# The first values of two head groups, summed together block by block in six banks

## The chip, the cores and the metric

The kernel runs on one core of a Trainium2 chip. The metric is the device time of one execution in microseconds (us). Before the change it is 1462.3 us, the median of three runs between 1461.91 and 1462.77.

The engines are named as the profile names them: PE is TensorE (matrix products and transposes) and PEld its weight loads; DVE is VectorE, ACT is ScalarE, POOL is GpSimd, and SP (SyncE) issues most of the transfers. Each engine takes its instructions strictly in the order of the program, and they wait for each other through semaphores. Transfers go from the memory outside the core (HBM) to the on-chip memory (SBUF); products are summed in PSUM, which has eight banks of 512 float32 columns.

## The reference, and what is computed

One layer of an encoder on x (1024 tokens by 1024 features): token mixing with two head groups side by side, cross-attention into 256 memory tokens, and a squared-ReLU MLP. Only its first lines matter here:

```python
h = rmsnorm(x, g_mix_pre[l])
proj = h @ w_in[l]          # fq fk fv f_logit cq ck cv
y_fox = forgetting_attention(fq, fk, fv, f_logit)
y_chk = chunked_relpos_attention(cq, ck, cv, rel_bias[l])
```

The change concerns the first products of the program: the values of four heads of each group, that is 256 columns of cv (called group 1, "chk") and 256 columns of fv with the 8 columns of the forget gate beside them (group 0, "fox", 264 columns), for all 1024 tokens.

## The kernel before, in words

**Numbers in two parts.** A float32 operand is split into a hi part (a copy rounded to the format that PE takes at full rate) and a lo part (the operand less its hi part). A product is then three products, hi·hi, hi·lo and lo·hi, summed in one bank; mm3 (L191 to L195) writes these three.

**Halves and blocks.** The 1024 tokens are two halves (th 0 and 1) of 512, each four token blocks (kb) of 128. The 1024 features over which is summed are eight contraction blocks (kc) of 128. A bank holds one token block of one group; it takes 8 contraction blocks of 3 products, 24 products. The first half's values are 4 token blocks of 2 groups, 192 products, and the second half's as many.

**The first half** does not wait for the norm. x is loaded transposed (xT), multiplied by the gain gmix alone and split (gained_hi on ACT at L1648, gained_lo on DVE at L1651). The norm's factor, one number per token, is applied when the values leave their bank: value_leave (L341) copies the hi part on ACT (L348), for group 0 the gate columns too (L350, fcol), and takes the lo part on DVE (L351).

The factor comes from sums of squares. For the first half, square (L1633) squares each block on ACT (L1636) and adds it up on DVE (L1638); when all eight are added, four small products with a column of 1/1024 (ssx, L1697) sum over the features, DVE adds epsilon (L1698) and POOL raises to the power -0.5 (L1699). For the second half ACT squares four row blocks of x with a running sum (L1705), and POOL does the rest (L1716, L1717). To scale the transposed x, the factors are turned into rows: transposes on PE (rr, L1725) and copies on ACT into rrows (L1726).

**The order of the first half.** Group 1 goes first: its four banks are filled side by side, contraction block by contraction block. Then group 0 bank by bank (values, L335): token block 0, ssx, token block 1, the eight turning transposes rr, token blocks 2 and 3. Group 1's banks are emptied while group 0's are filled. Weight pieces are split in value_split: group 1's hi parts on POOL (L316), group 0's on ACT (L318), all lo parts on DVE (L319).

**The second half and the norm.** normed (L1738) scales x on DVE (scaled, L1732), splits off the hi part on ACT (L1733) and takes the lo part on DVE (rest, L1736), for the eight blocks of the second half and then for those of the first half again, which later products use. Calls of value_leave stand at given places between these blocks. Group 1 is then summed over its four token blocks at once, and group 0 bank by bank.

**Transfers.** One piece of the first weights goes on ACT's queue, the rest on SP's: gmix, the two halves of the first xT pair, a weight piece, two xT pairs, a weight piece, the last xT pair, then group 0's weights with the rows of x between them.

**What follows.** stock holds the weights that come next: stock.load(3) issues three loads, stock.split_now(2) splits the first two (wq and wk: hi on ACT at L449, lo in two pieces on POOL at L458). attention_phase then writes the rest from a plan that keeps its own clock and starts at zero there; its first products are q, which read the first half's normalised x and wq. All of this part is written out by hand, so each engine's order is the order of the text.

**Warm-up.** 17 transposes of a constant (L1628) run on PE while the first data is on its way.

Of the kernel before, what the change touches and what calls it, by code (L numbers as in the profile page):

```python
# [14 lines left out]
F32 = mybir.dt.float32  # L15
# [120 lines left out]
def build(ctx, tc, nc, out, t):  # L136
# [155 lines left out]
    def value_raw(g, i, tag=None, halves=False):  # L292


        n, (a, b) = 264 if g == 0 else 256, VPARTS[g][i]
        shape = [P, b - a, n]
        raw = (wp.tile(shape, F32, tag="wraw", bufs=3, name=f"wrawv{g}{a}") if tag is None else
               p1.tile(shape, F32, tag=tag, bufs=2, name=f"wrawv{g}{a}"))
        src = t[f"w_v{g}"][a * P * n:b * P * n].rearrange("(p k n) -> p k n", p=P, n=n)
        if not halves:  # L300
            nc.sync.dma_start(raw, src)
            return raw
        h = (b - a) // 2
        return raw, [lambda j=j, q=q: q.dma_start(raw[:, j:j + h, :], src[:, j:j + h, :])
                     for j, q in ((0, nc.scalar), (h, nc.sync))]

    def value_split(g, raw, i, pieces=1, between=None):
        k, shape = raw.shape[1], list(raw.shape)
        if g == 1:
            wh, wl = (wp.tile(shape, F32R, tag=x, bufs=2, name=f"{x}v{i}") for x in ("whi", "wlo"))  # L310
        else:
            wh, wl = (u4(f"{x}v0{i}", shape) for x in ("whi", "wlo"))
        n = k // pieces
        for j in range(0, k, n):
            if between:
                nc.gpsimd.tensor_copy(wh[:, j:j + n, :], raw[:, j:j + n, :])  # L316
            else:
                nc.scalar.activation(wh[:, j:j + n, :], raw[:, j:j + n, :], AF.Copy)  # L318
            nc.vector.tensor_sub(wl[:, j:j + n, :], raw[:, j:j + n, :], f(wh[:, j:j + n, :]))  # L319
            if between and j == 0:  # L320
                between()
        return [(wh[:, j, :], wl[:, j, :]) for j in range(k)]

# [6 lines left out]

    def value_part(ps, w, kb, kc):
        act, cs = hT[kb // 4], slice((kb % 4) * P, (kb % 4 + 1) * P)
        mm3(ps, act.hi(kc, cs), act.lo(kc, cs), *w[kc], kc == 0, kc == KC - 1)

    def values(g, w, kb, tag):  # L335
        ps = value_bank(g, kb, tag)
        for kc in range(KC):
            value_part(ps, w, kb, kc)
        return ps
# [1269 lines left out]
    with tc.manual_schedule():  # L1609
        xt, xloads = load_pair(0, 0, True)  # L1610
        raw, wloads = value_raw(1, 0, halves=True)
        xT, raw1 = {0: [xt], 1: []}, [raw]
        gmix = const.tile([P, KC], F32, name="gmix")
        wloads[0]()
        early = const.tile([P, 1], F32, name="early")
        nc.scalar.activation(early, mhalf[:, 0:1], AF.Copy)
        nc.sync.dma_start(gmix, t["g_mix_pre"])
        xloads[0]()
        xloads[1]()
        wloads[1]()  # L1620
        xT[0] += [load_pair(0, 1), load_pair(0, 2)]
        raw1.append(value_raw(1, 1))
        xT[0].append(load_pair(0, 3))
        raw0 = [value_raw(0, 0)]
        vs = {g: value_tiles(g) for g in (1, 0)}
        warm = mm_tile([P, 4, P], "warm", "tr")
        for n in range(17):
            nc.tensor.transpose(warm[:, n % 4, :], ident, ident)  # L1628
# [11 lines left out]
        w1, w0, xr = [], [], []  # L1640

        def row(b):
            xr.append(p1.tile([P, D], F32, tag="sp", bufs=5, name=f"x{b}"))
            nc.sync.dma_start(xr[-1], t["x"][b * P:(b + 1) * P, :])

        def gained_hi(kc):

            nc.scalar.activation(hT[0].hi(kc), xT[0][kc // 2][:, kc % 2, :], AF.Copy, scale=gmix[:, kc:kc + 1])  # L1648
# [8 lines left out]

        gained_hi(0)
        w1 += value_split(1, raw1[0], 0, 2, lambda: (gained_lo(0), gained(1)))
        for kc in (2, 3):  # L1660
            gained(kc)
        for kc in (0, 1):
            square(kc)
        gained(4)
        w1 += value_split(1, raw1[1], 1, 2, lambda: gained(5))
        for kc in (2, 3):
            square(kc)
        for kc in (6, 7):
            gained(kc)
        first = [value_bank(1, kb, ("mm", "tr")[kb // 2]) for kb in range(4)]  # L1670
        for kc in range(KC):
            if kc > 1:
                for kb in range(4):
                    value_part(first[kb], w1, kb, kc)
                continue

            for n in range(3):
                for kb in range(4):
                    cs = slice(kb * P, (kb + 1) * P)
                    x = (hT[0].lo if n == 2 else hT[0].hi)(kc, cs)  # L1680
                    nc.tensor.matmul(first[kb], x, w1[kc][n == 1], start=kc == 0 and n == 0, stop=False)
        raw0 += [value_raw(0, 1, "bias"), None]
        for kc in (4, 5):
            square(kc)
        w0 += value_split(0, raw0[0], 0)
        w0 += value_split(0, raw0[1], 1)
        for b in (4, 5):
            row(b)
        raw0[2] = value_raw(0, 2)
        w0 += value_split(0, raw0[2], 2)  # L1690
        for kc in (6, 7):
            square(kc)
        ps0 = [values(0, w0, 0, "s")]
        rcols = [small.tile([P, 4], F32, tag="rs4", bufs=4, name=f"rx{th}") for th in range(2)]
        ps = mm_tile([P, 4], "ssx", "pv")
        for b in range(4):
            nc.tensor.matmul(ps[:, b:b + 1], sq[0][:, b * P:(b + 1) * P], o1024, start=True, stop=True)  # L1697
        nc.vector.tensor_scalar(rcols[0], ps, EPS, None, op0=ALU.add)  # L1698
        nc.gpsimd.tensor_tensor(rcols[0], rcols[0], mhalf[:, 0:4], op=ALU.pow)  # L1699

        ss1 = small.tile([P, 4], F32, tag="rs4", bufs=4, name="ssx1")
        junk = p1.tile([P, D], BF16, tag="o2", bufs=2, name="junk")

        def row_squares(b):
            nc.scalar.activation(junk, xr[b - 4], AF.Square, scale=1.0 / 32.0, accum_out=ss1[:, b - 4:b - 3])  # L1705

        for b in (6, 7):
            row(b)
        for p in range(4):
            xT[1].append(load_pair(1, p))  # L1710
        for b in (4, 5, 6):
            row_squares(b)
        row_squares(7)
        for kb in range(4):
            value_leave(1, kb, first[kb])
        nc.gpsimd.tensor_scalar(rcols[1], ss1, EPS, None, op0=ALU.add)  # L1716
        nc.gpsimd.tensor_tensor(rcols[1], rcols[1], mhalf[:, 0:4], op=ALU.pow)  # L1717
        ps0.append(values(0, w0, 1, "s"))
        value_leave(0, 0, ps0[0])

        rrows = p1.tile([P, 2, HT], F32, tag="bias", bufs=2, name="rrows")
        for th in (1, 0):
            tr = mm_tile([P, 4, P], f"rr{th}", "pv")
            for b in range(4):
                nc.tensor.transpose(tr[:, b, :], rcols[th][:, b:b + 1].to_broadcast([P, P]), ident)  # L1725
            nc.scalar.activation(rrows[:, th, :], tr.rearrange("p a b -> p (a b)"), AF.Copy)  # L1726
        nc.sync.dma_start(bfgt, t["b_fgt"])
# [10 lines left out]
        def normed(th, kcs, then={}):  # L1738

            for kc in kcs:  # L1740
                scaled(th, kc)
                if kc > kcs[0]:
                    rest(th, kc - 1)
                if kc in then:
                    then[kc]()
            rest(th, kcs[-1])

        for kb in (2, 3):
            ps0.append(values(0, w0, kb, "mm"))
# [717 lines left out]
```

## Time and profile before

| What | Value |
|---|---|
| Median of the runs | 1462.3 us |
| Profiled execution, span from first to last instruction | 1459.5 us |
| PE busy | 1447.7 us, 99% |
| DVE, ACT, POOL busy | 996.0, 820.7 and 421.0 us |
| First product of the values | 5.07 us |
| First product of the second half's values | 33.70 us |
| First product of q | 56.82 us |
| Mean granted clock of PE | 0.998 |

The profiled execution has a span of 1459.5 us; the runs' times count 2.8 us more around it. A row of the timeline gives start and duration in us, the engine, the line of the kernel, the operation, output and inputs by their names, and how many instructions are merged in it; in brackets stands how long the engine was idle before and what ended that. A row of the time table gives the stretch, its length, and the busy time of each engine with the number of its instructions, then the granted clock of PE (1.00 is full speed), the busy share of the DMA engines and their GB/s. A group row gives the summed busy time in us, the mean of one in ns, and the idle time before.

### The profile page before, as it was taken

The numbers are of one execution on the slowest core, as the hardware profiler recorded it, in microseconds if no ns is written. First come the engines' busy times: TensorE is split into PE (matmuls) and PEld (weight loads), VectorE is DVE, ScalarE is ACT, GpSimd is POOL, SyncE is SP. The second block draws the span as 40 slices with busy tenths as digits, with TensorE's granted clock in tenths as the row PEclk, the third lists the DMA queues.
The fourth block names the chain that finished last, engine by engine and source line by source line (L and its number), as shares of the span: only waits on it lengthen the run. The fifth ranks groups of instructions, "written<-read, shape, count | busy, mean of one in ns | idle before, by whom it ended". The sixth has DMA issues, their size and how long they took to land.

```text
span 1459.5 us, 21037 instructions
## 1 busy us (share of the span) xinstructions
PE 1447.7 (99%) x7265; PEld 1222.2 (84%) x7265; DVE 996.0 (68%) x1704; ACT 820.7 (56%) x1437; POOL 421.0 (29%) x520
## 2 busy tenths in 40 slices
PE   9999999999999999999999999999999999999998
PEld 8988888888889888888788888888888888888886
DVE  6777777767668847976873687765555666655576
ACT  6567677766677836555653465545555543444442
POOL 1245456555455301521332414343322000000021
PEclk9999999999999999999999999999999999999999
DMA  7132324321325584552541637754444785445565
GB/s 276 49 95 72 83 67 140 86 82 46 95 58 161 174 314 173 187 179 86 181 138 44 200 132 260 258 196 159 159 151 161 286 318 185 140 149 190 186 246 202
DMA packets 88987, 232.17 MB, mean 159 GB/s; under 512 B 10649, under 2 KB 14753, under 8 KB 88881
## 3 DMA queue, kind: packets, MB, share of 16 engines
q1 hardware_dynamic: 88736, 230.57, 47.6%
q8 instruction: 57, 0.93, 0.3%
q14 instruction: 50, 0.40, 0.1%
q10 hardware_dynamic: 144, 0.26, 0.1%
HBM read 167.30 MB, written 55.11 MB: 152 GB/s over the span
## 4 chain that ended last, share of the span: by engine, by line
PE 96%; DVE 2%; DMA 1%; ACT 1%; issue 0%; SPq 0%; DVEq 0%; ACTq 0%
PE pv L754 4%; PE fx L194 4%; PE fx L193 4%; PE fx L195 4%; PE ptr L711 4%; PE px L194 3%; PE fy L193 3%; PE px L195 3%; PE fy L195 3%; PE px L193 3%; PE fy L194 3%; PE mq L195 2%; PE q L193 2%; PE q L195 2%; PE q L194 2%; PE yw L193 2%
## 5 line engine op out<-in xcount | busy, mean ns | idle before, releaser
L717 DVE TENSOR_TENSOR phl<-ptr,phl 128x512 fp32r<-128x512 f32 (+1 forms) x152 | 92.5, 616 | 31.5 <-ACT phl L720 30.5
L2163 ACT ACTIVATE whif<-ra 128x1024 fp32r<-128x1024 f32 x37 | 39.2, 1061 | 130.3 <-PE fy L194 62.6
L2165 DVE TENSOR_TENSOR wlof<-ra,whif 128x1024 fp32r<-128x1024 f32 x37 | 45.3, 1225 | 91.7 <-ACT whif L2163 91.7
L720 ACT ACTIVATE phl<-ptr 128x512 fp32r<-128x512 f32 (+1 forms) x152 | 79.8, 540 | 40.3 <-PE ptr L711 38.5
L2285 POOL TENSOR_SCALAR rf<-sf 128x1 f32<-128x1 f32 x7 | 7.9, 1130 | 321.7 <-ACT jf L2266 321.4
L754 PE MATMUL pv<-phl,vs 128*128 128x512 f32 (+1 forms) x304 | 85.2, 366 | 0.2 <-DVE phl L717 0.2
L193 PE MATMUL fx<-vhif,whif 128*128 128x512 f32 x168 | 65.4, 389 | 0.0
L195 PE MATMUL fx<-vhif,wlof 128*128 128x512 f32 x168 | 65.4, 389 | 0.0
L194 PE MATMUL fx<-vlof,whif 128*128 128x512 f32 x168 | 65.4, 389 | 0.0
L754 PEld LDWEIGHTS pv<-phl,vs 128*128 128x128 f32 x304 | 55.2, 188 | 11.0 <-DVE phl L717 0.7
L2050 POOL TENSOR_TENSOR sc<-wf,wf 128x512 f32<-128x512 f32 x14 | 23.1, 1652 | 141.1 <-DMA wf<-in_w_ff 122.6
L768 POOL TENSOR_TENSOR o<-o 64x256 f32<-64x256 f32 x64 | 47.8, 747 | 53.1 <-DVE o L766 29.0
L193 PE MATMUL k<-hT_hi,whik 128*128 128x512 f32 x128 | 53.6, 419 | 0.0
L766 DVE TENSOR_TENSOR o<-pv,o 64x512 f32<-64x512 f32 x64 | 44.0, 688 | 13.5 <-ACT o L771 12.1
L193 PE MATMUL q<-hT_hi,whiq 128*128 128x512 f32 x128 | 51.6, 403 | 0.0
L193 PE MATMUL mq<-h2T_hi,whimq 128*128 128x512 f32 x128 | 51.4, 401 | 0.0
L195 PE MATMUL mq<-h2T_hi,wlomq 128*128 128x512 f32 x128 | 50.2, 392 | 0.2 <-DVE wlomq L455 0.2
L195 PE MATMUL k<-hT_hi,wlok 128*128 128x512 f32 x128 | 50.3, 393 | 0.0
L194 PE MATMUL k<-hT_lo,whik 128*128 128x512 f32 x128 | 50.3, 393 | 0.0
L195 PE MATMUL q<-hT_hi,wloq 128*128 128x512 f32 x128 | 50.2, 392 | 0.0
L194 PE MATMUL q<-hT_lo,whiq 128*128 128x512 f32 x128 | 50.2, 392 | 0.0
L194 PE MATMUL mq<-h2T_lo,whimq 128*128 128x512 f32 x128 | 50.1, 392 | 0.1
(696 smaller groups left out, 5014.5 us busy)
## 6 DMA issues: line engine op xcount, KB each, us to landing
ra<-gd SPq DMA_DIRECT2D x56, 512.0 KB, 3.8
wg<-in_w_ff SPq DMA_DIRECT2D x56, 512.0 KB, 5.6
wf<-in_w_ff SPq DMA_DIRECT2D x38, 512.0 KB, 3.9
gd<-s SPq DMA_DIRECT2D x48, 256.0 KB, 2.1
wrawmq<-in_w_mq SPq DMA_DIRECT2D x16, 512.0 KB, 4.3
gd<-u SPq DMA_DIRECT2D x32, 256.0 KB, 2.2
gd<-g SPq DMA_DIRECT2D x25, 256.0 KB, 2.2
wrawq<-in_w_qk SPq DMA_DIRECT2D x8, 512.0 KB, 4.4
```

What stands on the lines that cost most here:

```text
L193: nc.tensor.matmul(ps, lh, rh, start=start, stop=False, skip_group_check=more)
L194: nc.tensor.matmul(ps, lh, rl, start=False, stop=False, skip_group_check=more)
L195: nc.tensor.matmul(ps, ll, rh, start=False, stop=stop, skip_group_check=more)
L711: nc.tensor.transpose(tr[:, m, :], sp[:, k * P:(k + 1) * P], ident)
L717: flow.put("V", at, 0.7, lambda: nc.vector.tensor_sub(pl[:, live, :], tr[:, live, :], f(ph[:, live, :])), done)
L720: flow.put("S", flow.end, 0.6, lambda ph=ph, tr=tr, live=live: nc.scalar.activation(ph[:, live, :], tr[:, live, :], AF.Copy), split)
L754: nc.tensor.matmul(pv[:, :, qs_, :], v, hl[:, :, hs, :], start=c == 0 and turn == 0, stop=last)
L766: flow.put("V", at, 0.7, lambda: nc.vector.tensor_add(o2[own], pv[own, :, :, ::step], o2[own]), lambda end: (free["pv"].give(end), flow.pu ...
L768: free["pv"].give(end), flow.put("G", end, 0.8, lambda: nc.gpsimd.tensor_add(o2[own, 0], o2[own, 0], o2[own, 1]), store)))
L2050: eng.tensor_sub(sc[:, k1], r0[:, k0], r1[:, k0])
L2163: nc.scalar.activation(ah, ra, AF.Copy)
L2165: nc.vector.tensor_sub(al, ra, f(ah))
```

## The change

Both groups of first values are summed together: for each contraction block, the 12 products of group 1 (hi·hi of the four token blocks, hi·lo, lo·hi) and then the 12 of group 0. Group 1's four token blocks are 256 columns each and share two banks; group 0's have a bank each: six banks. ssx stands behind group 0's block 4, the turning transposes of the second half's factors between the groups in block 6, and those of the first half's behind block 6.

In the second half, blocks 0 to 3 of group 1 and then of group 0 are summed, and then blocks 4 to 7 of both. Since no bank of the first half is complete before its end, all eight calls of value_leave now stand inside normed(1): group 0's behind blocks 1, 2 and 3, group 1's behind blocks 4 and 5. The copies out of group 1's second half stand behind the whole normed(0), ahead of stock.split_now(2). Two copies out of one shared bank are kept apart: ACT's second copy waits for DVE's first.

All hi parts of value weights are cast on POOL. The first xT half is first in SP's queue, gmix second in ACT's, group 0's weights come in between the pieces of x, and the rows of x earlier. The first hi part of x is made in two halves of 256 columns. 14 warm-up transposes take the place of 17.

```diff
-        nc.sync.dma_start(gmix, t["g_mix_pre"])
+        l10[0]()
+        nc.scalar.dma_start(gmix, t["g_mix_pre"])
         xloads[0]()
+        l00[0]()
         xloads[1]()
-        wloads[1]()
+        l00[1]()
+        l10[1]()
...
-        for n in range(17):
+        for n in range(14):
...
+        def split_raw(g, raw, tiles, parts):
+            wh, wl = tiles
+            for x, y in parts:
+                nc.gpsimd.tensor_copy(wh[:, x:y, :], raw[:, x:y, :])
+                nc.vector.tensor_sub(wl[:, x:y, :], raw[:, x:y, :], f(wh[:, x:y, :]))
...
+        for c in (0, 256):
+            gained_hi(0, slice(c, c + 256))
+        split_raw(1, r10, w1t[0], ((0, 2),))
+        gained_lo(0)
+        split_raw(0, r00, w0t[0], ((0, 1),))
+        gained(1)
+        split_raw(0, r00, w0t[0], ((1, 3),))
+        split_raw(1, r10, w1t[0], ((2, 4),))
+        for kc in (0, 1):
+            square(kc)
+        gained(2)
+        gained(3)
+        split_raw(0, r01, w0t[1], ((0, 3),))
+        split_raw(1, r11, w1t[1], ((0, 2),))
+        for kc in (2, 3):
+            square(kc)
+        gained(4)
+        gained(5)
+        split_raw(1, r11, w1t[1], ((2, 4),))
+        for kc in (4, 5):
+            square(kc)
+        gained(6)
+        gained(7)
+        for kc in (6, 7):
+            square(kc)
+        split_raw(0, r02, w0t[2], ((0, 2),))
...
+        def value_pairs(g, kb0, tags):
+            if g == 0:
+                return [value_bank(0, kb0 + k, tags[k // 2]) for k in range(4)]
+            both = [mm_tile([P, 2, 256], f"v1_{kb0}{k}", tags[k]) for k in range(2)]
+            return [both[k // 2][:, k % 2, :] for k in range(4)]
+
+        def value_kc(g, banks, w, kb0, kc):
+            act = hT[kb0 // 4]
+            for n in range(3):
+                for k in range(4):
+                    cs = slice(k * P, (k + 1) * P)
+                    x = (act.lo if n == 2 else act.hi)(kc, cs)
+                    nc.tensor.matmul(banks[k], x, w[kc][n == 1],
+                                     start=kc == 0 and n == 0 and (g == 0 or k % 2 == 0),
+                                     stop=kc == KC - 1 and n == 2, skip_group_check=g == 1)
...
+        b1, b0 = value_pairs(1, 0, ("mm", "mm")), value_pairs(0, 0, ("s", "pv"))
+        for kc in range(KC):
+            value_kc(1, b1, w1, 0, kc)
+            if kc == 6:
+                turned_rows(1)
+            value_kc(0, b0, w0, 0, kc)
+            if kc == 4:
+                ps = mm_tile([P, 4], "ssx", "tr")
+                for b in range(4):
+                    nc.tensor.matmul(ps[:, b:b + 1], sq[0][:, b * P:(b + 1) * P], o1024, start=True, stop=True)
...
+            if kc == 6:
+                turned_rows(0)
...
+        normed(1, range(KC), {1: leave(0, b0, 0, 1), 2: leave(0, b0, 2), 3: leave(0, b0, 3),
+                              4: leave(1, b1, 0, 1), 5: leave(1, b1, 2, 3)})
+        c1, c0 = value_pairs(1, 4, ("tr", "tr")), value_pairs(0, 4, ("s", "pv"))
         bias_rows(0)
         normed(0, range(0, 4))
         stock.load(3)
+        for k0 in (0, 4):
+            for g, banks, w in ((1, c1, w1), (0, c0, w0)):
+                for kc in range(k0, k0 + 4):
+                    value_kc(g, banks, w, 4, kc)
+                if k0 and g:
+                    normed(0, range(4, KC))
+                    for call in leave(1, c1, 4, 5, 6, 7):
+                        call()
         bias_rows(1)
         stock.split_now(2)
+        for call in leave(0, c0, 4, 5, 6, 7):
+            call()
```

More of the change, by code (lines that the diff above doesn't have):

```diff
@@ L1713, in build, with turned_rows @@
[L1713 to L1719, printed above, removed]
         rrows = p1.tile([P, 2, HT], F32, tag="bias", bufs=2, name="rrows")
-        for th in (1, 0):
-            tr = mm_tile([P, 4, P], f"rr{th}", "pv")
+        def turned_rows(th):
+            tr = mm_tile([P, 4, P], f"rr{th}", "tr")
```

143 lines of the change are left out of this document (43 added, 100 removed).

## The prediction

> **What bounds the kernel now.** I read the page's first part, then the time table by stages, then TensorE's waits in the first 110 us, then each engine's order in the stage that is changed.
>
> ```profile
> span 1459.5 us, 21037 instructions
> ...
> PE 1447.7 (99%) x7265; PEld 1222.2 (84%) x7265; DVE 996.0 (68%) x1704; ACT 820.7 (56%) x1437; POOL 421.0 (29%) x520
> ```
> ```profile
> 5.07:33.70 28.63, 26.58 (x209) 1.00 0.86 320
> 33.70:56.82 23.12, 23.12 (x194) 1.00 0.00 1
> ```
> ```profile
> PE v L193 <- ACT hT_hi L1648: 0.9, 1, 0.9
> PE v L194 <- DVE wlov L319: 0.6, 1, 0.6
> PE v L1681 <- ACT hT_hi L1648: 0.5, 2, 0.3
> PE v L195 <- DVE hT_lo L1651: 0.2, 1, 0.2
> ```
>
> TensorE (PE) is busy 99% of the span, so an edit pays only where PE stands still, and costs wherever it makes PE stand still. The time table (length, PE busy, clock, share of DMA, GB/s) has the two halves of the first values: 5.07 to 33.70, with the gaps of the third fence (inputs not split yet), and 33.70 to 56.82, with none. The second half is 192 products in 23.12 us: 0.1204 each, 1.445 for the 12 products of one group and one contraction block, 2.89 for both groups. All that follows is one dense order, so what the first product of q loses or gains arrives at the end of the span unchanged.
>
> **Start.**
> ```profile
> 1.34 3.51 PE L1628 MATMUL warm<-ident 128*128 128x128 f32 x17 [1.34 <-POOL ident masks.py:199]
> 5.07 0.71 PE L1681 MATMUL v<-whiv,hT_hi 128*128 128x256 f32 x4 [0.22 <-ACT hT_hi L1648]
> ```
> ```profile
> 0.72 0.39 SPq L1617 DMA_DIRECT2D gmix<-in_g_mix_pre  x1
> 1.17 0.89 SPq L272 DMA_DIRECT2D xT<-in_xT  x2
> ```
> ```profile
> 4.21 0.72 ACT L1648 ACTIVATE hT_hi<-xT,gmix 128x512 fp32r<-128x512 f32 x1 [1.56 <-DMA xT<-in_xT]
> ```
> x goes ahead of gmix on SP, 0.45 us earlier (0.72 for 1.17); gmix now queues behind the first weights on ACT's queue and gates the same instruction, so the gain is between 0 and 0.45. The first hi part in halves lets PE start after some 0.45 of the 0.72. First product at about 4.45: 0.6 earlier (bounds 0.2 to 0.8). Three transposes less cost nothing as long as the clock is up by then; 14 end near 4.4.
>
> **The waits of the head.**
> ```profile
> 23.07 1.05 PE L1697 MATMUL ssx<-o,sqx 128*128 128x1 f32 x8
> 26.98 1.09 PE L1725 MATMUL rr<-ident,rx 128*128 128x128 f32 x8
> ```
> 28.63 less 23.12 of products, 1.05 of ssx and 1.09 of rr leaves 3.4 us lost before 33.70. Now each block holds PE 2.89 us instead of 1.445, and SP brings a block's x and both weights in about the time that x and one weight took, or little more; I leave 0.5 of the 3.4 (two waits like the smallest above, and block 2's low part). Without a new wait the first half would end at 33.70 - 0.6 - 2.9 = 30.2.
>
> **The new wait: the squares.** ssx now stands on PE behind block 4 of 8, not behind all of group 1 and a bank of group 0. PE gets there at 4.45 + 10 x 1.445 + 0.4 = 19.3. It waits for the last of the seven additions of squares on VectorE.
> ```profile
> 9.44:23.02 13.58, 13.02 (x18) 1.00 0.88 333
> ```
> ```profile
> 9.44 1.42 DVE L1651 SCALAR_TENSOR_TENSOR hT_lo<-xT,gmix,hT_hi 128x512 fp32r<-128x512 f32 x2 [0.52 <-ACT hT_hi L1648]
> ...
> 11.71 1.10 DVE L1651 SCALAR_TENSOR_TENSOR hT_lo<-xT,gmix,hT_hi 128x512 fp32r<-128x512 f32 x1
> 12.73 1.09 DVE L319 TENSOR_TENSOR wlov<-wrawv,whiv 128x512 fp32r<-128x512 f32 x1
> ...
> 19.13 2.49 DVE L319 TENSOR_TENSOR wlov<-wrawv,whiv 128x792 fp32r<-128x792 f32 x3
> 21.54 1.48 DVE L1638 TENSOR_TENSOR sqx<-sqx,sqx 128x512 f32<-128x512 f32 x2
> ```
> ```profile
> 7.46 0.73 POOL L316 CAST whiv<-wrawv 128x512 fp32r<-128x512 f32 x1 [3.42 <-DMA wrawv<-in_w_v]
> 11.30 1.99 POOL L316 CAST whiv<-wrawv 128x512 fp32r<-128x512 f32 x2 [3.10 <-DMA wrawv<-in_w_v]
> ```
> Before, VectorE goes from 9.44 to the last addition at 23.02 with 18 instructions and 0.56 of idle, so it is the bound of that work, and the work stays. In its new order the 17 instructions from the low part of the second weight piece to that addition are the same list less a 792 and the 528 (0.98 and 0.70 of the 2.49 for three, moved ahead or behind), plus one 512 (0.69): 12.6 us. Casts on GpSimd slow it: while two ran (11.30 to 13.29) two VectorE instructions took 1.10 and 1.09 for about 0.71 (1.42 for two), 0.38 per 512 columns. ScalarE's three casts of group 0 move to GpSimd; 792 + 528 columns fall into this stretch: +1.0. The piece it starts with lands behind 0.4 MB more than at 7.46 (1.2 us at the 320 GB/s of the first row) and is cast by 9.4. End: 9.4 + 12.6 + 1.0 = 23.0; bounds 20.6 (earlier piece, no idle, no slowing) and 24. PE waits 3.7 us (1.3 to 4.7), with block 5 and all behind it in its queue. The first half ends at 30.2 + 3.7 = 33.9, about where it ended before: what the head gains, this wait takes back.
>
> The Trainium skill ("SBUF — State Buffer", "SBUF: two separate sides") calls the port that VectorE and GpSimd share an exclusive lock, held for the whole instruction; by that rule a cast would add its full time alone (0.61 to 0.73 per 512 columns), and the squares would end near 23.9, not 23.0. The trace shows both slowed and neither stopped, so I keep 0.38.
>
> **The second half: VectorE is late.**
> ```profile
> L353 ACT ACTIVATE vs<-v 128x256 fp32r<-128x256 f32 x7 | 2.3, 378 | 0.0
> L348 ACT ACTIVATE vs<-v,rx 128x256 fp32r<-128x256 f32 x3 | 1.4, 458 | 0.0
> ```
> ```profile
> L1732 DVE SCALAR_TENSOR_TENSOR xT<-xT,gmix,rrows 128x512 f32<-128x512 f32 x16 | 11.7, 746 | 0.2 <-ACT rrows L1726 0.2
> L1736 DVE TENSOR_TENSOR hT_lo<-xT,hT_hi 128x512 fp32r<-128x512 f32 x16 | 11.0, 688 | 0.3
> L356 DVE TENSOR_TENSOR vs<-v,vs 128x256 fp32r<-128x256 f32 x6 | 2.3, 419 | 0.7 <-ACT fcol L355 0.7
> L351 DVE SCALAR_TENSOR_TENSOR vs<-v,rx,vs 128x256 fp32r<-128x256 f32 x4 | 1.9, 484 | 1.7 <-ACT fcol L350 1.7
> ```
> ```profile
> 28.29:55.46 27.17, 24.39 (x42) 1.00 0.13 52
> ```
> ```profile
> 54.29 1.06 ACT L449 ACTIVATE whiq<-wrawq 128x1024 fp32r<-128x1024 f32 x1
> ```
> ```profile
> 55.44 2.81 POOL L458 TENSOR_TENSOR wloq<-wrawq,whiq 128x512 fp32r<-128x512 f32 x2 [28.52 <-ACT whiq L449]
> ```
> ```profile
> 57.28 0.39 PE L195 MATMUL q<-hT_hi,wloq 128*128 128x512 f32 x1
> ```
> Normalising both halves of x (32 instructions) and 10 value copies kept VectorE 27.17 us, 28.29 to 55.46. The hi part of wq followed on ScalarE and its low part on GpSimd, 0.5 us before PE wanted it: that chain has no more slack than that. Before, five copies were done and four blocks scaled by 33.70. Now no bank is whole until the first half ends (T), and the code puts blocks 0 and 1 ahead of the first copies and the rest behind them; VectorE does two blocks and stands waiting for T.
>
> From T, in VectorE's order to the last low part: 8 copies, 14 scalings, 15 low parts. Back to back each costs 0.08 less than its duration (1.42 for two of 0.75): 8 x 0.41 + 14 x 0.66 + 15 x 0.61 = 21.7. Idle: 0.8 before the first two copies, 0.6 before each of the next two (1.7 for three above), 1.0 for each pair of group 1, whose shared bank makes ScalarE's second copy wait for VectorE's first (0.46 + 0.5), 1.0 in the scalings: 5.0. So T + 26.7. Then group 1's last four copies pass between the engines in turn (0.42 and 0.38 each; three on VectorE, and ScalarE's two between and after them: 0.35 + 0.4 + 0.4 + 0.4 + 0.35): +1.9. The hi part of wq stands behind them: +1.0; half of its low part (2.81 for two): +1.5. The third product of q starts at T + 31.1.
>
> PE on its way loses 2.4 us waiting for the low parts of blocks 1 to 3 (the copies stand ahead of them; 0.5 + 0.9 + 0.95), ends the values at T + 23.1 + 2.4 = T + 25.5, and then stands 4.1 us for wq and 1.0 for its low part. With T = 33.9: 65.0 against 57.28, +7.7 us. Bounds: T from 31.5 to 34.9, the chain from 29.2 (the idle of the pairs gone) to 32: +3.4 to +9.6.
>
> **The clock.**
> ```profile
> 1.34:4.34 3.00, 3.00 (x14) 3.00 (x15) 0.26 (x1) 1.43 (x3) 0.61 (x1) 1.00 0.82 250
> ...
> 1452.76:1455.00 2.24, 0.00 (x1) 0.00 (x0) 1.25 (x5) 0.98 (x3) 0.30 (x1) 1.00 0.36 134
> 1455.00:1459.50 4.50, 0.00 (x0) 0.00 (x0) 1.31 (x2) 0.00 (x0) 0.00 (x0) 0.50 0.31 117
> ```
> PE's last product ends at 1452.76; 2.24 us later the granted clock (third column from the right) is 0.50. At the start 14 of the 17 transposes took the first 3.00 us, 0.21 each, and the other three the last 0.51. A stand of 4 us therefore costs some 3 us at half speed, 1.5 lost; for the one at q, part of it falls into the 1.0 us wait: +1.3 (0 to 2.3). For the 3.7 us at the squares I take none (0 to 1.5).
>
> The Trainium skill ("TensorE: Matmul & The Clock Gate", "What's actually happening") halves the clock after one idle window of about 3.4 us of a free-running counter. By it the wait at q, over one window, is likely to be caught and the one at the squares may be: the time would be 1472.8 with both. Here 2.24 us sufficed once.
>
> Sum: +7.7 + 1.3 = +9.0 on the profiled span of 1459.5, that is 1468.5; the median of the runs, 1462.3, stands 2.8 above that span, and so 1471.3.
>
> **Rivals.** (1) Faster: VectorE keeps up. The head gains 0.6 + 2.9 and nothing takes it back: 1458.8. It decides where the third product of q starts before 57.28, so T must be under 26.2 with the chain as summed; PE's products alone put T at 29.7. Against it also the 0.5 us of slack. (2) No change: all idle in the chain closes (T + 26.5) with T near 31: 57.5 against 57.28, 1462 to 1463. For it: the squares could end at 20.6. (3) Smaller loss: the squares are ready nearly in time and the clock holds; T 31.5, chain 29.5: +3.7, 1466.0. (4) The clock falls at both waits: 1472.8.
>
> **How the numbers follow.** The forecast with (4), 1468 to 1474: 0.76. (3), 1465.3 to 1468: 0.14. (2) 0.06, (1) 0.04. A measurement of this kernel tells 0.2%, 2.9 us, from no change. So faster 0.04, same 0.06, slower 0.90. The range 1465.5 to 1474.0 takes in the lower bounds of (3) and both clocks.
>
> **What would show it.** PE idle at ssx with VectorE's square addition as releaser, near 19 to 23, and the first half ending near 33.9; PE waits for low parts early in the second half; then about 4 us on the hi part of wq and 1 on its low part; VectorE idle just ahead of T; a granted clock of 0.5 near 62. I am wrong if VectorE's additions end by 20, if ScalarE reaches wq by T + 23, or if later work absorbs a late q.

## The result and the profile after

The changed kernel takes 1470.97 us, the median of five runs between 1469.91 and 1471.55; the kernel before, run beside it, 1462.13 (1461.51 to 1462.77). The ratio is 1.0059, with a 95% interval of 1.0047 to 1.0071: 8.8 us slower. The forecast was 1471.3, in a range of 1465.5 to 1474.0.

The changed kernel's page begins with these lines (in the second, busy time, share and number of instructions of each engine):

```profile
span 1468.1 us, 21038 instructions
...
PE 1451.1 (99%) x7262; PEld 1224.2 (83%) x7262; DVE 999.2 (68%) x1705; ACT 819.5 (56%) x1435; POOL 423.8 (29%) x524
```

The span is 8.6 us longer than before (1459.5). TensorE's waits in the first 75 us of the changed kernel (line that waited, what released it, total us, how often, the longest):

```profile
PE q L193 <- ACT whiq L407: 4.1, 1, 4.1
PE v L1692 <- DVE hT_lo L1736: 1.7, 3, 0.7
PE v L1692 <- POOL whiv L1572: 1.4, 1, 1.4
PE warm L1627 <- POOL ident masks.py:199: 1.3, 1, 1.3
PE ssx L1720 <- DVE sqx L1637: 0.4, 1, 0.4
```

The waits of the old head (the part of the program up to the end of the first half) are gone. In their place stand a later first product, a small wait at the squares, three waits for low parts in the second half, and 4.1 us at q. PE's own order of time in the changed kernel:

```profile
6.03 1.20 PE L1692 MATMUL v<-whiv,hT_hi 128*128 128x256 f32 x4 [1.44 <-POOL whiv L1572]
...
22.61 1.05 PE L1720 MATMUL ssx<-o,sqx 128*128 128x1 f32 x8 [0.35 <-DVE sqx L1637]
...
33.13 0.65 PE L1692 MATMUL v<-whiv,hT_hi 128*128 128x256 f32 x4
...
62.90 0.79 PE L193 MATMUL q<-hT_hi,whiq 128*128 128x512 f32 x1 [4.07 <-ACT whiq L407]
...
64.26 0.80 PE L195 MATMUL q<-hT_hi,wloq 128*128 128x512 f32 x1
...
68.19 1.03 PE L479 MATMUL ftr<-ident,fcol 128*8 128x128 f32 x8
```

So T, the end of the first half, is 33.13 (before: 33.70), and q's third product starts at 64.26 (before: 57.28): +6.98. The transposes of the gates' columns (ftr), which follow q's twelfth product, start 8.62 later than in the kernel before:

```profile
59.57 1.03 PE L521 MATMUL ftr<-ident,fcol 128*8 128x128 f32 x8
```

The products between them cost 1.64 more. From there to the end of the span the difference stays between 8.3 and 8.6. The loss is made between 33 and 68 us, and nothing later gives it back.

The instructions on which the wait at the squares and the one at q end (VectorE's last additions of squares and its last low parts of x, then ScalarE's hi part of wq):

```profile
21.08 1.48 DVE L1637 TENSOR_TENSOR sqx<-sqx,sqx 128x512 f32<-128x512 f32 x2
...
58.47 1.47 DVE L1736 TENSOR_TENSOR hT_lo<-xT,hT_hi 128x512 fp32r<-128x512 f32 x2
```
```profile
61.80 1.05 ACT L407 ACTIVATE whiq<-wrawq 128x1024 fp32r<-128x1024 f32 x1
```

VectorE's last low part of x ends at 59.94, T + 26.8; the hi part of wq ends at 62.85; between the two, ScalarE still makes the copies out of group 1's banks. The time table of the changed kernel around q (stretch, length, PE's busy time and instructions, granted clock, share of DMA, GB/s):

```profile
57.35:60.77 3.42, 1.48 (x13) 1.00 0.00 0
60.77:64.18 3.41, 1.22 (x2) 0.50 0.05 7
64.18:67.59 3.41, 3.33 (x8) 0.50 0.24 70
67.59:71.00 3.41, 3.41 (x21) 1.00 0.83 244
```

The clock falls to half in the stand and comes back at 67.59: those are the 1.64 us.

### The profile page after: what moved, and what is told of

The parts are those of the page before. It is cut to its first block, busy times and chain, and to the rows that moved or that the text cites. A ratio compares the mean times of both kernels' runs of the same rounds, so it can differ in the third digit from the quotient of the medians.

```text
span 1468.1 us, 21038 instructions
## 1 busy us (share of the span) xinstructions
PE 1451.1 (99%) x7262; PEld 1224.2 (83%) x7262; DVE 999.2 (68%) x1705; ACT 819.5 (56%) x1435; POOL 423.8 (29%) x524
## 4 chain that ended last, share of the span: by engine, by line
PE 94%; issue 2%; DVE 2%; DMA 1%; ACT 1%; SPq 0%; POOL 0%; DVEq 0%; POOLq 0%; ACTq 0%
PE pv L712 4%; PE fx L194 4%; PE fx L193 4%; PE fx L195 4%; PE ptr L669 4%; PE fy L194 3%; PE px L194 3%; PE px L195 3%; PE px L193 3%; PE fy L193 3%; PE fy L195 3%; PE q L195 2%; PE q L193 2%; PE k L193 2%; PE q L194 2%
## 5 line engine op out<-in xcount | busy, mean ns | idle before, releaser
L193 PE MATMUL yw<-whiwo,yT_hi 128*128 128x512 f32 x128 | 50.2, 392 | 0.0
```

Of the source, the lines that this page charges most:

```text
L193: nc.tensor.matmul(ps, lh, rh, start=start, stop=False, skip_group_check=more)
```

## Experiments on the second half

Times are medians; the kernel before, run beside them, was at 1462.04 (both runs that move the split of wq alone, PE kept busy, 24 transposes), at 1461.56 (low parts first, casts on ScalarE, gain vector first, squares a block later) and at 1461.5 to 1461.9 (the last three).

**The split of wq early.**

```diff
                 if k0 and g:
+                    stock.split_now(1)
                     normed(0, range(4, KC))
...
         bias_rows(1)
-        stock.split_now(2)
+        stock.split_now(1)
```

> The changed kernel with the split of wq's first block (its hi part on ScalarE, its low part on GpSimd) put ahead of the normalising of blocks 4 to 7 instead of behind the last value copies. My theory: in the changed kernel PE stands 4.1 us for the hi part and 0.14 more for the low part only because they stand last in ScalarE's order; with them ready, q's first product follows the last value product (58.8) and the third starts at 59.9 to 60.5 instead of 64.26, limited at the most by the last low part of x (59.9). With no stand the clock stays up, which saves the 1.6 us that the ten slow products cost. So 4.2 + 1.6 = 5.8 us less than the changed kernel: 1465.2. Rival A, VectorE is the bound whatever the order: PE then waits as long for low parts of x among q's products: within 1 us of the changed kernel. Rival B, later work absorbs a late q: within 1 us of the changed kernel although q starts 4 us earlier.

Measured: 1469.39 us, 1.6 less instead of 5.8. The third product of q came at 59.51, even before the time I gave, and still most of the gain was lost: waits of this run (the first 75 us) are

```profile
PE ftr L479 <- DVE vs L314: 1.7, 1, 1.7
...
PE ftr L479 <- ACT fcol L313: 1.3, 1, 1.3
```

PE runs 12 products of q and then stands 3.1 us for the last value copies, which free the banks for the gates' transposes and hold their columns; in that stand the clock falls too. Group 0's last copies began 1.5 us later than in the changed kernel (65.15 for 63.69): T came 0.4 later, and beside GpSimd's low part of wq one scaling and one low part of x took 1.79 and 1.77 us on VectorE instead of about 0.75 and 0.69. Neither theory had it: wq was only the first of two things that stood at the end of the same chain. Rival B falls (an earlier q alone is not absorbed later, it meets the next wait), and rival A has the right engine but the wrong wait.

**The split of wq ahead of the last copies.**

```diff
                     normed(0, range(4, KC))
+                    stock.split_now(1)
                     for call in leave(1, c1, 4, 5, 6, 7):
```

> The changed kernel with the same split put between the last scaling of x and the four value copies of group 1. Theory: the hi part starts at 59.1 and ends at 60.2, PE stands 1.4 us for it and about 1.2 more for the first half of the low part; the third product of q starts at 61.5, 2.7 us earlier than in the changed kernel. Whether the clock falls in a stand of 1.4 us is what this run tells beside: with the clock up 1470.97 - 2.7 - 1.6 = 1466.7, with the clock down 1468.3. If the copies were not what holds the hi part back, the time would be that of the changed kernel.

Measured: 1467.0 us, q's third product at 61.65 (expected 61.5). Here the copies lose little, and q's first product comes at 60.29 instead of 62.90. The hi part's place behind group 1's copies cost these 2.6 us (the sum had 1.9 for those copies). The clock did fall in the profiled execution, for one window (below), though the longest stand was 1.4 us. Three of the five executions took 1466.5 to 1467.0 us and two, the profiled one among them, 1467.8 to 1467.9; whether the clock fell in the others too, no trace shows.

**PE kept busy in the stand at q.**

```diff
+        cover = mm_tile([P, 4, P], "cover", "mm")
+        for n in range(36):
+            nc.tensor.transpose(cover[:, n % 4, :], ident, ident)
         bias_rows(1)
         stock.split_now(2)
```

> The changed kernel with 36 transposes of the identity matrix between the last value product and the first product of q: PE is busy where it stood, nothing else changes. Theory: the stand lets the clock fall and ten products of q then run at 0.43 instead of 0.23 us; with the stand filled they run at 0.23 and the time is 1.6 us less, 1469.4. The third product of q still starts near 64.3. Rival: the first products of q are slow for another reason (the GpSimd work or the loads beside them), and the time stays at 1471.0.

Measured: 1469.65 us, 1.3 less. In this run's order the products of q follow each other at full pace, with q as late as in the changed kernel:

```profile
58.93 4.09 PE L1765 MATMUL cover<-ident 128*128 128x128 f32 x36
63.16 0.50 PE L193 MATMUL q<-hT_hi,whiq 128*128 128x512 f32 x1
...
64.86 0.40 PE L193 MATMUL q<-hT_hi,whiq 128*128 128x512 f32 x1
```

From q's third product to the gates' transposes PE takes 2.43 us here, 3.93 in the changed kernel and 2.29 before. So the clock costs 1.5 to 1.64 us at this place, and it comes from the stand, not from work beside q. The 1.3 of the medians are less firm: the two kernels' runs overlap (1469.32 to 1470.73 against 1469.91 to 1471.55), and the two profiled spans differ by 0.2 only, because this run's has small stands at 559 and 884 us that the other lacks.

**Low parts of x ahead of the copies.**

```diff
-        normed(1, range(KC), {1: leave(0, b0, 0, 1), 2: leave(0, b0, 2), 3: leave(0, b0, 3),
-                              4: leave(1, b1, 0, 1), 5: leave(1, b1, 2, 3)})
+        normed(1, range(KC), {3: leave(0, b0, 0, 1), 4: leave(0, b0, 2), 5: leave(0, b0, 3),
+                              6: leave(1, b1, 0, 1), 7: leave(1, b1, 2, 3)})
```

> The changed kernel with two more blocks of x normalised ahead of the first value copies (the copies stand behind blocks 3 to 7 instead of 1 to 5). Theory: VectorE works in the 1.5 us in which it stood for the end of the first half, and the low parts of blocks 1 to 3 no longer stand behind copies, so PE's three waits for them (1.7 us in all) go; the last value product starts near 57.2 instead of 58.7, the hi part of wq and the third product of q come 1.5 us earlier (62.8), PE's stand at q stays near 4.1: 1469.5. Rival, the copies are the bound: they end later, PE waits for their banks in the second half instead, and the time is 1471 or more.

Measured: 1469.3 us, as expected, but not for the reason given. This run's waits:

```profile
PE q L193 <- ACT whiq L407: 1.9, 1, 1.9
PE ssx L1720 <- DVE sqx L1637: 1.9, 1, 1.9
PE v L1692 <- DVE vs L309: 1.8, 1, 1.8
```

The three waits for low parts (1.7) went, and the rival's wait for the banks of the copies came in their place (1.8). VectorE's chain was 1.0 shorter (q's third product 30.14 behind T instead of 31.13). The stand at q shrank by 2.2: PE arrived 1.4 later, and the hi part of wq came 0.7 earlier. q's third product gained 0.75 and not the 1.5 expected, and the span of the profiled execution is 0.8 shorter, not 1.7. The agreement of the median is a coincidence.

## Experiments on the first half

**More transposes at the start.**

```diff
-        for n in range(14):
+        for n in range(24):
             nc.tensor.transpose(warm[:, n % 4, :], ident, ident)
```

> The changed kernel with 24 transposes of the identity matrix at the start instead of 14, so that PE is busy until its first value product (6.03) instead of standing 1.4 us. Theory: the first 15 value products then run at 0.12 instead of 0.215 us, PE arrives at the sums of squares 1.5 us earlier (20.7), but the last square addition ends at 22.5 as before, so PE waits there 1.9 us instead of 0.4: the first half ends at the same 33.1 and the time is the same, 1471.0 (within 0.3). Rival: the squares follow PE and come earlier too: 1469.5.

Measured: 1472.64 us, 1.7 more by the medians and 2.8 by the spans of the profiled executions (1470.9 for 1468.1), outside both expectations. The mechanism is the one expected: the first products run at full pace, PE then waits 1.9 us at the squares instead of 0.4, and T is 33.53, 0.4 later only (the first product was 0.3 later, behind the transposes). The rest came at q. This run's time table, in the columns above:

```profile
60.37:63.78 3.41, 0.48 (x2) 1.00 0.00 0
63.78:67.19 3.41, 2.88 (x8) 0.50 0.20 28
67.19:70.61 3.42, 3.42 (x13) 0.50 0.68 208
```

The clock stayed at half for 6.8 us of products instead of 4.7, and the gates' transposes were slow too, which with the 0.4 makes 1.6 at this place; two smaller stands at 562 and 887 us, which the changed kernel's profiled execution lacks, add 1.1 of the 2.8. Why those differ I did not settle.

**Group 0's casts back on ScalarE.**

```diff
-                nc.gpsimd.tensor_copy(wh[:, x:y, :], raw[:, x:y, :])
+                if g == 0:
+                    nc.scalar.activation(wh[:, x:y, :], raw[:, x:y, :], AF.Copy)
+                else:
+                    nc.gpsimd.tensor_copy(wh[:, x:y, :], raw[:, x:y, :])
```

> The changed kernel with the hi parts of group 0's weights (four casts) on ScalarE again instead of GpSimd; those of group 1 stay on GpSimd. Theory: VectorE's instructions that ran beside these casts (1.1 to 1.3 us for 0.74) run at their own pace, about 1.3 us less up to the last square addition, and it ends at 21.2 to 21.6 if ScalarE has room for 2.6 us of casts. PE's wait at the sums of squares (0.4 to 1.9, by when the clock rises at the start) becomes smaller by at most that: 1469.7 to 1471.0. Rival: the casts wait for their loads on ScalarE and hold back the squares and the hi parts of x queued behind them: squares end later than 22.5, and the time is above 1471.

Measured: 1470.29 us (1468.81 to 1472.78). The eight low parts of x on VectorE between 4 and 24 us, first in the changed kernel, then in this run (busy us in all, mean ns of one):

```profile
L1644 DVE SCALAR_TENSOR_TENSOR hT_lo<-xT,gmix,hT_hi 128x512 fp32r<-128x512 f32 x8 | 7.0, 904 | 0.0
```
```profile
L1647 DVE SCALAR_TENSOR_TENSOR hT_lo<-xT,gmix,hT_hi 128x512 fp32r<-128x512 f32 x8 | 5.7, 745 | 0.1
```

That is the 1.3 us of the expectation. The last square ends at 21.71 instead of 22.56 (22.56 to 23.03 in the seven profiled executions with the changed kernel's loads and casts), and T comes at 32.30. So the casts on GpSimd did push the squares back, by 0.85 or more; ScalarE had the room. That the whole is faster is not shown: the gates' transposes come 0.9 earlier, but the two spans are equal (1468.1), with small stands at 560 and 982 us in between, and the runs overlap.

**The gain vector's load first.**

```diff
         l10[0]()
-        nc.scalar.dma_start(gmix, t["g_mix_pre"])
...
+        nc.sync.dma_start(gmix, t["g_mix_pre"])
         xloads[0]()
```

> The changed kernel with the load of the gain vector put first on SyncE's queue again, ahead of x, instead of second on ScalarE's. Theory: the gain vector lands near 3.0 instead of 5.3 and x and the first weights near 4.1 and 3.4 to 4.5 instead of 4.7 and 4.9; the first value product starts at 5.0 to 5.5 instead of 6.0. The end of the first half hangs on the last square addition; this moves only as far as VectorE starts earlier, at most 0.8: 1470.2 to 1471.0. Rival: the weights and x land at the same times (the queue order of x, not the gain vector, spread them), and the first product stays at 5.8 to 6.1.

Measured: 1473.61 us, 2.6 more; the first product came at 4.99, as expected, and the time was missed. Loads in the first 12 us (queue, KB, us from issue to landing), in the changed kernel and in this run:

```profile
wrawv<-in_w_v SPq DMA_DIRECT2D x1, 396.0 KB, 5.3
wrawv<-in_w_v ACTq DMA_DIRECT2D x1, 256.0 KB, 4.2
...
gmix<-in_g_mix_pre ACTq DMA_DIRECT2D x1, 4.0 KB, 4.1
```
```profile
wrawv<-in_w_v SPq DMA_DIRECT2D x1, 396.0 KB, 7.2
wrawv<-in_w_v ACTq DMA_DIRECT2D x1, 256.0 KB, 2.7
...
gmix<-in_g_mix_pre SPq DMA_DIRECT2D x1, 4.0 KB, 2.4
```

With the 4 KB of the gain vector behind it on ScalarE's queue, the first weight piece takes 4.2 us instead of 2.7; with them ahead of x on SyncE's queue, the 396 KB piece behind takes 1.9 longer. The late pieces hold VectorE: the last square ends at 23.47, 0.9 later, and PE stands 2.9 us at the sums of squares. In that stand the clock falls, here too: it is at half from 24.68 to 28.10, which costs 1.5 us, and T comes at 35.58, 2.45 later. This run is the prediction's own picture of the first half, an early first product and a long wait at the squares, and in it the fourth rival holds: the clock falls at both waits.

**The sums of squares one block later** (with the 24 transposes).

```diff
-            if kc == 4:
+            if kc == 5:
...
-                nc.gpsimd.tensor_tensor(rcols[0], rcols[0], mhalf[:, 0:4], op=ALU.pow)
                 nc.gpsimd.tensor_scalar(rcols[1], ss1, EPS, None, op0=ALU.add)
                 nc.gpsimd.tensor_tensor(rcols[1], rcols[1], mhalf[:, 0:4], op=ALU.pow)
+                nc.gpsimd.tensor_tensor(rcols[0], rcols[0], mhalf[:, 0:4], op=ALU.pow)
```

> The run with 24 transposes at the start, and with the sums of squares put one contraction block later (behind block 5 instead of 4; on GpSimd the other half's factors first). Theory: in that run PE waited 1.9 us for the squares; one block is 2.9 us of products, so the wait goes and the first half ends at 31.6 instead of 33.5. VectorE then starts its copies 1.5 us earlier (it stood 1.5 us for them), and everything up to q follows: the third product of q at 63.1 instead of 64.65, time 1471.1 against 1472.64 of that run. Rival: VectorE's copies are held by something else (the factors of the rows), and q starts at 64.3 or later, with PE waiting longer for low parts of x: the time of that run, 1472.6.

Measured: 1469.85 us, 2.8 less than the run with 24 transposes (1.5 expected); T at 31.99, 0.4 later than expected, and q's third product at 63.11, as expected. The wait at the squares is gone and everything up to q follows T. By the traces the gates' transposes come 1.5 earlier than in the run with 24 transposes; most of the rest is that these transposes run at full pace here and that the stands at 562 and 887 us are absent.

## Experiments with all of it together

**The order mended.** 24 transposes, the squares behind block 5, and:

```diff
+        for kc in (6, 7):
+            row_squares(kc - 2)
+            square(kc)
...
+        normed(1, range(KC), {2: leave(0, b0, 0, 1, 2, 3), 4: leave(1, b1, 0, 1), 6: leave(1, b1, 2, 3)})
...
+                    first = stock.to_split.pop(0)
+                    stock.hi(first)
+                    stock.lo(first, nc.vector)
+                    seen[first] = 0.0
+                    normed(0, range(4, KC), {5: leave(1, c1, 4, 5), 6: leave(1, c1, 6, 7)})
```

> The changed kernel with what the runs so far pointed to, taken together: 24 transposes at the start, the sums of squares behind block 5 (on GpSimd the other half's factors first), two of the four row squares on ScalarE ahead of the last two squares, three blocks of x normalised ahead of the first copies, the split of wq's first block ahead of blocks 4 to 7 with its low part on VectorE, and group 1's last copies among those blocks. Theory: every stand of PE from the value products to q had an owner in the order of VectorE and ScalarE, not in the six banks. The first half ends at 31.6 to 32.0, VectorE begins to scale at 27.3 instead of 29.2 and keeps up, the second half takes its 23.1 us, and the third product of q starts at 55.2 to 56.0, against 64.26 in the changed kernel and 57.28 in the kernel before; PE may stand about 1 us at the transposes of the gates' columns behind q's 12th product. The time: 1462.3 minus 1.3 to 2.1 plus 0 to 1: 1460.2 to 1462.0. Rival: the six banks bring all copies at once and VectorE cannot place them: stands of 3 us or more remain and the time is above 1464.

Measured: 1465.52 us, ratio to before 1.0027 (1.0016 to 1.0039). q's third product came at 55.92, within the expectation, 8.3 us earlier than in the changed kernel and 1.4 earlier than before. The stand at the gates' transposes was 3.1 us and not 1:

```profile
PE ftr L479 <- ACT fcol L313: 3.1, 1, 3.1
```

The time is the one that the rival named, above 1464 with a stand of 3 us. Whether the six banks or only the place of group 0's last copies in the order make that stand, the next run tells.

**Group 0's last copies earlier.** The four lines above on `first` now stand behind the products of both groups, with this order:

```diff
+        normed(1, range(KC), {2: leave(0, b0, 0, 1, 2, 3), 5: leave(1, b1, 0, 2, 1, 3)})
...
+        for call in leave(1, c1, 4, 6, 5, 7):
+            call()
...
+        normed(0, range(4, KC), {6: leave(0, c0, 4, 5, 6, 7)})
```

> The run that took all together, with group 0's last copies (and with them the gates' columns) ahead of the last two blocks of x and of the hi part of wk on ScalarE, group 1's last copies ahead of blocks 4 to 7, and copies from a shared bank alternating between the two banks. Theory: q's third product stays near 55.9; the 3.1 us that PE stood at the transposes of the gates' columns, and the 1.6 us of slow products behind it, go, but for 0 to 0.5: 1465.5 - 4.7 = 1460.8, or to 1461.3; that would be 0.5 to 0.9 us under the kernel before. Rival: VectorE, busy almost without a break from 28 to 61, is the bound now, and PE waits 1 us or more for the low parts of blocks 6 and 7 among q's products: 1462 to 1464.

Measured: 1460.85 us against 1461.48 for the kernel before; ratio 0.9994 (0.9985 to 1.0003). The waits of this run's first 110 us:

```profile
PE warm L1627 <- POOL ident masks.py:199: 1.3, 1, 1.3
PE v L1699 <- DVE hT_lo L1741: 0.4, 1, 0.4
PE q L193 <- DVE kl L806: 0.3, 1, 0.3
```

Six banks summed block by block do not cost 9 us: with the same summation and another order of VectorE's, ScalarE's and GpSimd's work, q's third product comes at 55.63 and PE hardly stands. Against before that is 1.65 us earlier, of which 1.1 are left when the first scores start (PE stands 0.3 for `kl` at 83.8) and nothing at the end of the two profiled executions (spans 1459.6 and 1459.5): 0.65 more go at a short stand for ScalarE's copies at 551 us and the rest at one for VectorE at 974. So a lead of this size was absorbed by later work. What the same reordering would give the kernel before was not run.

**Two small stands taken out.** 21 transposes, and

```diff
+        normed(1, range(KC), {2: leave(0, b0, 0, 1), 4: leave(0, b0, 2, 3), 5: leave(1, b1, 0, 2, 1, 3)})
```

> The last run with two small stands taken out: 21 transposes at the start instead of 24 (the last of them ended 0.3 to 0.4 us after the first value product could start), and the copies of blocks 2 and 3 of group 0 behind block 4 of x instead of ahead of block 3 (PE stood 0.4 us for the low part of block 3). Theory: q's third product at 54.9 to 55.2 instead of 55.63, time 1460.85 - 0.5 to 0.7 = 1460.2 to 1460.4. Rival: PE waits for the copies of blocks 2 and 3 at the start of group 0's second half instead (their banks), and the time stays at 1460.9 or above.

Measured: 1460.91 us, before 1461.92; ratio 0.9994 (0.9984 to 1.0003). q's third product came at 55.20, 0.4 earlier, and the time did not follow; the lead of 2.1 us over the kernel before at the gates' transposes is gone at 1180 us, again in short stands. Both last versions lie 0.6 to 1.0 us under the kernel before by their medians, and both intervals contain 1: that either beats it is not shown.

## Why the prediction was right, point by point

**Start: wrong.** The step was "the gain is between 0 and 0.45 ... first product at about 4.45: 0.6 earlier (bounds 0.2 to 0.8)". It came at 6.03, 1.0 later than before. The bound excluded a loss without a reason: I had counted the place of each load in its queue, and not how long the loads take in the new places. The first product needs the first weights' cast and the first hi part of x, which needs the gain vector. In the changed kernel both were late (GpSimd, then ScalarE):

```profile
4.92 0.97 POOL L1572 CAST whiv<-wrawv 128x512 fp32r<-128x512 f32 x2 [3.63 <-DMA wrawv<-in_w_v]
```
```profile
5.38 1.52 ACT L1641 ACTIVATE hT_hi<-xT,gmix 128x256 fp32r<-128x256 f32 x3 [2.24 <-DMA gmix<-in_g_mix_pre]
```

The gain vector landed 4.1 us after its issue, against 2.3 before, and ScalarE stood for it until 5.38; its first half of the hi part ended at 5.89, 0.14 ahead of the product. The list of waits above names GpSimd's cast for this wait; but the cast that the first product needs, the first of the two, had ended at 5.53, and the second ends at 5.89 as well. In the runs that move the split of wq, with the same start, the wait ends on ScalarE's hi part (`hT_hi`). So the gain vector was the gate, as the prediction had it, and the weights beside it were late too, 4.2 us instead of 2.7. That the load's place does both is shown by the run that moved it. How 4 KB can do it stays open; ScalarE's queue carried 288 packets in place of 144.

**Clock at the start: wrong.** "Three transposes less cost nothing as long as the clock is up by then": in the profiled execution it was not, and 15 products took 3.36 us, 0.22 each. Whether it is up differs between executions: with the same 14 transposes the first rise of the clock on record is at 9.57, 10.84 and 10.78 us (the changed kernel and the two runs that move the split of wq alone), but at 4.99, 5.08 and 5.23 in three others (PE kept busy, low parts first, casts on ScalarE).

**The squares: the mechanism right, the wait mis-sized by what the first two did.** The last addition ended at 22.56 (predicted 23.0, 20.6 to 24), and GpSimd's casts were shown to slow VectorE about as much as reckoned (1.3 against 1.0). PE came at 22.3 and not at 19.3, so it waited 0.4 and not 3.7. With the clock up from the start the wait was 1.9, with an early first product 2.9, with the sums a block later nothing. PE cannot pass the squares, so T hardly depends on when PE arrives as long as it comes before them: 33.13, against 33.9 predicted. Two errors of the head, 3.0 us together, went into a wait of 3.7 that was there to swallow them. That they were no larger, and that the wait left over was too short to let the clock fall, is luck.

**The second half: right.** T + 26.7 for VectorE's last low part (measured T + 26.8), T + 31.1 for q's third product. Over the runs that leave the second half's order alone:

| run | T | q's third product | difference |
|---|---|---|---|
| the changed kernel | 33.13 | 64.26 | 31.13 |
| PE busy in the stand | 33.37 | 64.52 | 31.15 |
| 24 transposes | 33.53 | 64.65 | 31.12 |
| casts on ScalarE | 32.30 | 63.42 | 31.12 |
| gain vector first | 35.58 | 66.69 | 31.11 |
| squares a block later | 31.99 | 63.11 | 31.12 |

T moves over 3.6 us and the difference over 0.04: VectorE's and ScalarE's written order behind T is what sets q. PE's loss at the low parts was 1.7 (predicted 2.4), the stand for the hi part of wq 4.1 (4.1); the third product followed the first by 1.36 instead of 0.46, 0.9 more (1.0).

**The clock: right in kind, +1.64 against +1.3,** and none at the squares, as taken, but only because the wait there shrank to 0.4 us: in the run with the long wait, 2.9, the clock fell there too and cost 1.5; with waits of 1.9 it did not.

**Sum:** +6.98 + 1.64 = 8.62 on the span, predicted +9.0; 1468.1 against 1468.5: T was 0.8 earlier than predicted and the clock took 0.3 more. The last step, 2.8 us from the span to the median, is not a cost around the span, as the section on the kernel before has it: each run counts about 1.8 us above its own span (1461.35 for 1459.5, 1469.91 for 1468.1), and the rest is that the profiled execution was 1.0 faster than the median. For the changed kernel it happened to be 1.1 faster. Of the rivals, "faster" needed T under 26.2 and "no change" needed T near 31: T was 33.13. "Smaller loss" failed at the stand at q, 4.1 us, and "the clock falls at both waits" at the short wait at the squares; with the gain vector first it came true, at 1473.61 us.

**What the prediction did not see:** that the hi part of wq was not the only work at the end of that chain. The gates' columns stood there too, 3 us behind, and were found only when wq was moved.

## What to carry to other kernels

When a change makes several results ready at the same moment, find the engine that has to take them away and write down its order from that moment on: here a list of 37 VectorE instructions, with the idle of each exchange, gave the start of the next stage to 0.1 us, while the start of the kernel, reckoned from places in queues, was missed by 1.6. A step ahead of a wait that holds for another reason can be missed by that much without harm, unless the longer wait makes the clock fall; otherwise it shows only when the wait is taken away. And a late item at the end of an engine's order has others behind it: before moving one forward, look at who waits for the next.

## What was not expected of the hardware

**Changes of the clock lie on a grid, and a part of a window is enough.** In each profiled execution all changes of the granted clock lie whole multiples of 3.413 us apart, with another offset in each execution. Cut along that grid, the windows just ahead of a fall and of no fall are (same columns as above; first the run with the split ahead of the copies, then low parts first, then casts on ScalarE):

```profile
58.57:61.98 3.41, 1.38 (x6) 1.00 0.00 0
```
```profile
39.21:42.63 3.42, 1.62 (x13) 1.00 0.01 2
42.63:46.04 3.41, 3.41 (x18) 0.50 0.00 0
```
```profile
56.43:59.84 3.41, 1.59 (x14) 1.00 0.00 0
59.84:63.25 3.41, 0.73 (x2) 1.00 0.04 6
```

Before the end of the program the clock fell behind eleven windows, in which PE was busy 0.09 to 0.47 of the time, and not behind windows from 0.47 up. The edge is not sharper than that: it fell behind one window with 1.62 of 3.41 us of products (second table) and not behind one with 1.59 (third table), so it lies about there, or the modelled ends of the products blur it. It rose behind windows with 0.88 and more, and stayed low behind the window with 2.88 of 3.41 us, 0.84, in the run with 24 transposes. The Trainium skill ("TensorE: Matmul & The Clock Gate", "What's actually happening") has the clock halve after one idle window of about 3.4 us; the window's length agrees, but a window more than half idle was enough here: stands of 1.4 and 0.6 us in one window cost a fall. What a stand costs therefore depends on where it lies on the grid, which differs between executions.

**A load of 4 KB moved others by more than a microsecond,** as told above: 1.5 us for the 256 KB ahead of it on its own queue, 1.9 for a 396 KB piece behind it on the other. It holds in every profiled execution: with the gain vector second on ScalarE's queue the first weight piece took 4.2 to 4.4 us and the 396 KB piece 4.7 to 5.4 in all eleven; with it first on SyncE's, 2.7 and 7.2.
